# Down projection of four token tiles by seven block products instead of eight, weight sums by accumulating DMAs, the next modulation on TensorE

## The chip, the cores and the metric

The kernel runs on one core of a Trainium2 chip. A core has TensorE (PE, matrix products into PSUM), VectorE (DVE), ScalarE (ACT), GpSimd (POOL), SyncE (SP, which issues DMAs here) and 16 DMA engines. The metric is the time of one execution on the device, in microseconds (us); the kernel before takes 1401.62 us (median of three, 1400.32 to 1407.0).

## The reference

A two-layer network (D = 1024) works on 512 latent tokens and 128 context tokens. Each layer modulates and normalises, mixes tokens in four ways, and ends with a dense SwiGLU whose hidden width is 2816. The change lies in the last product and in the modulation that the next layer begins with:

```python
def modulation(cond, w_ada, b_ada):
    m = jax.nn.silu(cond) @ w_ada + b_ada
    ...
def swiglu(h, w_gate_up, w_down):
    g, u = jnp.split(h @ w_gate_up, 2, axis=-1)
    return (jax.nn.silu(g) * u) @ w_down
...
    h2 = rmsnorm(x, g_pre_ffn) * (1.0 + scale2) + shift2
    x = x + gate2 * rmsnorm(swiglu(h2, w_gate_up, w_down), g_post_ffn)
    return x, ckv, k_rope
```

The arithmetic is float32, with `w_down` of 2816 x 1024 for each layer.

## The kernel before, in words

**Products.** Every large product is three matmuls (`mm3`): each operand is split into a rounded part and a rest (`split`: ACT copies the rounded part, DVE subtracts it for the rest), and high x high, high x low and low x high are added in PSUM. A weight passes through `load`: SP issues a DMA into one of three `raw` buffers of 128 x 1024 float32 (512 KB), then ACT and DVE split it into one of eight `w` buffers. A `raw` buffer is free for the next DMA when its split has ended.

**Tokens.** The 640 tokens are five tiles of 128: 0 to 3 latent, 4 context. Hidden activations `hid` lie with the features on partitions: 22 slices of 128 features, tokens in the order 0 1 4 3 2. The last two slices are in a `w` buffer (`wk848` in layer 0).

**Down projection.** `w_down` makes the output in two halves of 512 columns. For each half, 11 loads of two slices are split, `hsplit` splits the two slices of all 640 tokens (128 x 1280), and five PSUM banks, one for each tile, collect 22 x 3 matmuls of 512 columns: 660 matmuls for a layer. In the second half the last three loads are kept (`tail`), so that the tiles end one after another. Behind each tile ACT squares and sums it, DVE multiplies it by the gate, POOL takes the root (`rsq`), DVE adds it to the residual (`postnorm`), SP stores it; in layer 0 the next norm (`prenorm`: ACT square, POOL root, two DVE scalings in `normalise`, eight transposes on TensorE) follows, and then the first products of the next layer's `w_in` (`pd`, 352 columns, in `pd_all`).

**Modulation.** The modulation of the next layer is made during layer 0's `w_down` by `queue_ada_v`: 16 steps, each one DMA of 512 KB into a `raw` buffer and two multiply-adds of 128 x 1024 on DVE; at the end of each half TensorE sums over partitions with four matmuls on `ones` and four transposes. In other places of the kernel the same kind of product is made on TensorE (`queue_gates`: 8 steps of four narrow matmuls, `ada_mm`, line 282).

**Order.** Instructions are written in the order in which TensorE is to run them. `clk` counts planned TensorE time, and background steps (`bg`) are put in at planned intervals; each engine runs its own queue in that order, with waits between queues. All DMAs of the kernel before are issued by SP, in order.

Of the kernel before, what the change touches and what calls it, by code (L numbers as in the profile page):

```python
# [10 lines left out]
F32 = mybir.dt.float32  # L11
R = mybir.dt.float32r
# [5 lines left out]
N = NS + NP  # L18
# [48 lines left out]
def layout(i):  # L67
# [21 lines left out]
    col = lambda v: np.repeat(v.reshape(L, 8, 128).transpose(0, 2, 1)[..., None], 2, 3).reshape(L, 128, 16)  # noqa: E731  # L89
# [30 lines left out]
    wd = a["w_down"].reshape(L, FF, 2, 512)  # L120
    o["w_dn"] = np.stack([kpack(wd[:, :, h], 2) for h in range(2)], 1)
# [6 lines left out]
# ---------------------------------------------------------------- chip  # L128
AFF = ("ssss", "aaaa")
START = (("aass",) * 5, ("aass",) * 5)  # L130
class Trunk:
    """The instructions are written in the order that the tensor engine runs them. A chain that has
    to wait for other engines is a generator: it yields the time (us of the tensor engine) until its
    next part is worth issuing, and the matmuls of other chains are issued meanwhile."""
# [8 lines left out]
    # -- order of issue  # L143
# [41 lines left out]
    # -- allocation  # L185
# [22 lines left out]
    # -- small things  # L208
# [13 lines left out]
    def mm3(self, out, l, r, start, stop):  # L222
        (lh, ll), (rh, rl) = l, r
        mm = self.nc.tensor.matmul
        mm(out, lh, rh, start=start, stop=False)  # L225
        mm(out, lh, rl, start=False, stop=False)  # L226
        mm(out, ll, rh, start=False, stop=stop)  # L227
# [13 lines left out]
    def rsq(self, ms, two=False):  # L241
        """(ms + eps)^-1/2 of each column, or of the sum of two."""
# [17 lines left out]
    # -- set-up  # L260
# [24 lines left out]
    def new_mod(self, l, r):  # L285
        """[shift, scale][k][c, c_ctx] of one norm, features on the partitions."""
# [50 lines left out]

    def queue_ada_v(self, l, r):
        """The same with the products on the vector engine; the tensor engine adds up the partitions."""
# [851 lines left out]
```

## Time and profile before

| what | before |
|---|---|
| time, median of three | 1401.62 us (1400.32 to 1407.0) |
| span of the profiled execution | 1403.1 us |
| PE busy | 1364.4 us (97%) |
| DVE busy | 1024.7 us (73%) |
| ACT busy | 620.6 us (44%) |
| POOL busy | 218.8 us (16%) |
| DMA | 180.61 MB, 129 GB/s on average |

The profiled execution is one run of the program; its span, from the first to the last instruction, is the only time of it that the profile has, and it stands 1.5 us above the median of the three timed runs. Busy times are of single engines and overlap. The granted clock is the clock of TensorE as a share of full speed. A line such as `L225 PE MATMUL ps<-w,hs` names the source line, the engine, the operation, and the tiles written and read; the time in square brackets is how long the engine had been idle, and what it waited for.

### The profile page before, as it was taken

The page shows a single profiled execution, that of the slowest core. Times are in us where ns is not written, and L with a number is a line of the kernel's source. Part 1 is how long each engine was busy: PE and PEld are TensorE (multiplying, and loading weights), DVE is VectorE, ACT ScalarE, POOL GpSimd, SP SyncE. Part 2 cuts the span into 40 slices and gives each one's busy share as a digit, 9 for nine tenths or more (in the row PEclk, how much of TensorE's full clock was granted, in tenths as well). Part 3 has the DMA queues.
Part 4 walks back from the last instruction along what each step waited for, and adds up shares of the span by engine and source line. Part 5 has one row for each costly group of instructions (what it writes and reads, how often), then busy time and mean ns, then how long its engine had stood idle before and what let it go on. Part 6 is the DMA issues. An engine that isn't in the chain of part 4 may idle for free. (4 is left out here: it accounts for less than half of the span.)

```text
span 1403.1 us, 21451 instructions
## 1 busy us (share of the span) xinstructions
PE 1364.4 (97%) x8320; PEld 1227.3 (87%) x8320; DVE 1024.7 (73%) x1722; ACT 620.6 (44%) x1210; POOL 218.8 (16%) x218
## 2 busy tenths in 40 slices
PE   5899999999999999999999999999999999999998
PEld 2788977899999999887888897878999999998886
DVE  3789476599988987978177966757998898782433
ACT  4543275564444444316173324736544444362410
POOL 1101121111222111000031202302021122140001
PEclk9999999999999999999999999999999999999999
DMA  9455246233222233655245533653122222342131
GB/s 374 164 173 184 91 143 236 98 114 99 85 88 76 91 91 108 194 181 166 85 155 167 183 115 122 189 188 135 61 90 91 91 90 77 106 135 77 59 105 75
DMA packets 50613, 180.61 MB, mean 129 GB/s; under 512 B 6784, under 2 KB 7680, under 8 KB 49488
## 3 DMA queue, kind: packets, MB, share of 16 engines
q1 hardware_dynamic: 50512, 179.25, 38.9%
q8 instruction: 65, 1.06, 0.3%
q14 instruction: 36, 0.29, 0.1%
HBM read 168.55 MB, written 10.68 MB: 128 GB/s over the span
## 5 line engine op out<-in xcount | busy, mean ns | idle before, releaser
L210 ACT ACTIVATE w<-raw 128x512 fp32r<-128x512 f32 (+2 forms) x228 | 186.4, 824 | 315.1 <-PE ps L227 204.0
L216 DVE TENSOR_TENSOR w<-raw,w 128x512 fp32r<-128x512 f32 (+2 forms) x228 | 215.9, 950 | 96.7 <-ACT w L210 93.5
L225 PE MATMUL ps<-T,w 128*128 128x320 f32 x640 | 197.8, 309 | 0.0
L226 PE MATMUL ps<-T,w 128*128 128x320 f32 x640 | 197.8, 309 | 0.0
L227 PE MATMUL ps<-T,w 128*128 128x320 f32 x640 | 197.8, 309 | 0.0
L225 PE MATMUL ps<-b,w 128*128 128x320 f32 x608 | 188.0, 309 | 0.0
L226 PE MATMUL ps<-b,w 128*128 128x320 f32 x608 | 187.9, 309 | 0.0
L227 PE MATMUL ps<-b,w 128*128 128x320 f32 x608 | 187.9, 309 | 0.0
L213 DVE TENSOR_TENSOR s<-ps,s 128x320 f32<-128x320 f32 (+1 forms) x304 | 142.3, 482 | 52.1 <-PE ps L227 50.8
L225 PE MATMUL ps<-w,hs 128*128 128x512 f32 x440 | 172.6, 392 | 0.2 <-ACT hs L210 0.2
L227 PE MATMUL ps<-w,hs 128*128 128x512 f32 x440 | 171.4, 390 | 0.3 <-DVE hs L216 0.3
L226 PE MATMUL ps<-w,hs 128*128 128x512 f32 x440 | 171.7, 390 | 0.0
L910 POOL TENSOR_TENSOR hid<-s 128x320 f32<-128x320 f32 x72 | 88.3, 1230 | 400.5 <-ACT s L210 369.6
L216 DVE TENSOR_TENSOR w<-sw,w 128x512 fp32r<-128x512 f32 x160 | 127.4, 814 | 0.0
L355 DVE SCALAR_TENSOR_TENSOR acc<-raw,cond,acc 128x1024 f32<-128x1024 f32 x84 | 108.4, 1318 | 17.9 <-DMA raw<-in_ada 17.9
L225 PEld LDWEIGHTS ps<-T,w 128*128 128x128 f32 x640 | 120.1, 188 | 0.0
L226 PEld LDWEIGHTS ps<-T,w 128*128 128x128 f32 x640 | 120.1, 188 | 0.0
L227 PEld LDWEIGHTS ps<-T,w 128*128 128x128 f32 x640 | 120.1, 188 | 0.0
L226 PEld LDWEIGHTS ps<-b,w 128*128 128x128 f32 x608 | 114.1, 188 | 0.1
L225 PEld LDWEIGHTS ps<-b,w 128*128 128x128 f32 x608 | 114.1, 188 | 0.1
L227 PEld LDWEIGHTS ps<-b,w 128*128 128x128 f32 x608 | 114.1, 188 | 0.0
L210 ACT ACTIVATE w<-sw 128x512 fp32r<-128x512 f32 x160 | 96.3, 622 | 34.7 <-PE ps L227 20.0
(219 smaller groups left out, 2674.0 us busy)
## 6 DMA issues: line engine op xcount, KB each, us to landing
raw<-in_w_gu SPq DMA_DIRECT2D x88, 512.0 KB, 3.5
raw<-in_ada SPq DMA_DIRECT2D x80, 512.0 KB, 4.1
raw<-in_w_dn SPq DMA_DIRECT2D x44, 512.0 KB, 3.6
ada<-in_ada SPq DMA_DIRECT2D x8, 1024.0 KB, 14.3
raw<-in_w_out SPq DMA_DIRECT2D x16, 512.0 KB, 4.9
xs<-work SPq DMA_DIRECT2D x14, 512.0 KB, 2.6
work<-xs SPq DMA_DIRECT2D x13, 512.0 KB, 4.4
raw<-in_w_b SPq DMA_DIRECT2D x12, 512.0 KB, 4.4
```

Source lines behind the costliest of these rows:

```text
L210: self.nc.scalar.activation(out, in_, f, **kw)
L213: self.nc.vector.tensor_tensor(out, x, y, op=op)
L216: self.nc.vector.tensor_tensor(lo, src, hi.bitcast(F32), op=ALU.subtract)
L225: mm(out, lh, rh, start=start, stop=False)
L226: mm(out, lh, rl, start=False, stop=False)
L227: mm(out, ll, rh, start=False, stop=stop)
L355: nc.vector.scalar_tensor_tensor(acc[:, s], raw, c, acc[:, s], op0=ALU.mult, op1=ALU.add)
L910: eng.tensor_tensor(h[:, ::-1] if c else h, x, y, op=ALU.mult)
```

## The change

`w_down` is written anew. The four latent tiles form two pairs, A (0, 1) and B (3, 2); the features form even and odd slices; the output has two halves. This 2 x 2 by 2 x 2 product is made by Winograd's form of Strassen's seven products, in seven passes over 11 slices (five groups of two slices and one of one slice, `w_dt`), and tile 4's plain products ride along in four of them: p1 (tiles 0, 1, 4), p5 (2 tiles), p6 (2), p3 (3), p7 (3), p2 (3), p4 (2): 18 tile products x 11 slices x 3 = 594 matmuls of 512 columns for a layer. Sums of weight blocks are made by accumulating DMAs, issued from GpSimd: `V`, in three `w` buffers, holds one block at p1 and is added to for p5, p6 and p4; for p7 a freshly loaded `raw` is added to and then split. Differences of activations are made on DVE (`dd`), partial sums in PSUM are copied by ACT (`cc`, `u2`) and added in `finish`. Tiles 0, 1 and 4 are finished early in p4 (`left`), tiles 3 and 2 at its end. In layer 0 `queue_ada_p` takes the place of `queue_ada_v`: 8 steps, each two DMAs of 512 KB and four narrow matmuls on TensorE, then four transposes. `pd_all` takes the tiles in the order 0, 1, 4, 3, 2. The host stores `w_down` by even and odd slices.

```diff
-                self.bg, self.bg_last = [(5.48, f) for f in q], self.now + 2.68
+                mod1, q = self.queue_ada_p(l + 1, 0)
+                self.bg, self.bg_last = [(8.0, f) for f in q], self.now + 8.0
...
-        for t in range(NT):
+        for t in (0, 1, 4, 3, 2):
             self.join(pre[t])
...
+        def add(dst, e, h, g):
+            nc.gpsimd.dma_start(out=dst, in_=dram(e, h, g), accum_op=ALU.add)
+
+        def fresh(g, e, h):
+            r = self.raw()[:, 0 : cnt(g) * 512]
+            nc.sync.dma_start(out=r, in_=dram(e, h, g))
+            return r
...
+        def p1(g):
+            into(g, 0, 0)
+            w = wsplit(g, vg(g))
+            add(vg(g), 0, 1, g)
+            h = xsplit(g, [x(g, 0)[:, :, A4]])
+            self.tt(d(g), x(g, 1)[:, :, D4], x(g, 0)[:, :, D4], ALU.subtract)
+            return h, w
+
+        go(p1, [(bA[0], 0, True, True), (bA[1], 128, True, True), (b4[0], 256, True, False)])
...
+        def p6(g):
+            w = wsplit(g, vg(g))
+            add(vg(g), 1, 0, g)
+            s = d(g)[:, :, 128:384]
+            nc.vector.scalar_tensor_tensor(s, s, -1.0, x(g, 0)[:, :, 0:256], op0=ALU.mult, op1=ALU.subtract)
+            return xsplit(g, [s]), w
...
+        def p7(g):
+            r = fresh(g, 0, 1)
+            add(r, 1, 1, g)
+            w = wsplit(g, r)
+            h = self.Q([2, 2, 384], R, "hs")
+            k = cnt(g)
+            s = self.S()[:, 0 : k * 256].rearrange("p (k n) -> p k n", k=k)
+            self.tt(s, x(g, 0)[:, :, 0:256], x(g, 0)[:, :, B4], ALU.subtract)
+            self.split(h[:, 0, 0:k, 0:256], h[:, 1, 0:k, 0:256], s)
+            self.split(h[:, 0, 0:k, 256:384], h[:, 1, 0:k, 256:384], x(g, 0)[:, :, 256:384])
+            return h, w
...
+        def left():
+            for t in (0, 1, 4):
+                begin(t)
+                if t < 4:
+                    finish(t, 0, bC[t], cc[:, 0, t, :])
+                else:
+                    finish(4, 0, b4[0])
+                end(t)
+
+        later.append(left)
+
+        def p4(g):
+            return xsplit(g, [x(g, 1)[:, :, B4]]), wsplit(g, vg(g))
+
+        steps = run(p4, [(bA[0], 0, None, True), (bA[1], 128, None, True)], tail=2)
```

On POOL, at the start of layer 0's down projection, the queue before held the last hidden products and then the roots of the tiles (`mso` are the sums of squares):

```order
L910 TENSOR_TENSOR wk848_5582<-s857_5624 128x5x64
L910 TENSOR_TENSOR wk848_5582<-s849_5583 128x320
L910 TENSOR_TENSOR wk848_5582<-s869_5745 128x5x64
L910 TENSOR_TENSOR wk848_5582<-s866_5716 128x320
L246 TENSOR_SCALAR rs1991_6724<-mso0885_5834 128x1
```

In the changed kernel the same stretch of POOL's queue begins so (`wk896`, `wk901` and `wk906` are the three buffers of `V`), and ends with the sums for p7:

```order
L944 TENSOR_TENSOR wk848_5582<-s857_5624 128x5x64
L944 TENSOR_TENSOR wk848_5582<-s849_5583 128x320
L1064 DMA wk896_5845<-in_w_dn 128x1024 x2
L944 TENSOR_TENSOR wk848_5582<-s869_5745 128x5x64
L1064 DMA wk901_5900<-in_w_dn 128x1024
L944 TENSOR_TENSOR wk848_5582<-s866_5716 128x320
L1064 DMA wk901_5900<-in_w_dn 128x1024
L1064 DMA wk906_5955<-in_w_dn 128x1024
L1064 DMA wk906_5955<-in_w_dt 128x512
```

24 sums now stand between the hidden products and the roots, and two hidden products of the last slice stand behind sums of p1.

On SP, in the middle of layer 0's down projection, weights and modulation shared the three `raw` buffers before, each released by DVE:

```order
L255 DMA raw936_6238<-in_w_dn 128x1024 [waits DMAHW5_49,DVE_49]
L349 DMA raw939_6252<-in_ada 128x1024 [waits DMAHW6_49,DVE_49]
L255 DMA raw940_6280<-in_w_dn 128x1024 [waits DMAHW7_49,DVE_49]
L349 DMA raw943_6291<-in_ada 128x1024 [waits DMAHW0_49,DVE_49]
L349 DMA raw944_6322<-in_ada 128x1024 [waits DMAHW1_49,DVE_49]
```

Now, at the end of p3 (`raw970` is its last group) and in p7 (`raw973`, `raw977`, `raw985`, `raw989`, `raw993` are its groups 0 to 4):

```order
L364 DMA raw968_6409<-in_ada 128x1024 [waits DMAHW2_49,PE_49]
L364 DMA raw969_6411<-in_ada 128x1024 [waits DMAHW3_49,DVE_49]
L1068 DMA raw970_6426<-in_w_dt 128x512 [waits DMAHW4_49,DVE_49]
L1068 DMA raw973_6444<-in_w_dn 128x1024 [waits DMAHW7_49,DVE_49]
L1068 DMA raw977_6475<-in_w_dn 128x1024 [waits DMAHW5_49,PE_49]
L364 DMA raw981_6491<-in_ada 128x1024 [waits DMAHW6_49,PE_49]
L364 DMA raw982_6493<-in_ada 128x1024 [waits DMAHW2_49,PE_49]
L1068 DMA raw985_6532<-in_w_dn 128x1024 [waits DMASW2_49,DVE_49]
L1068 DMA raw989_6563<-in_w_dn 128x1024 [waits DMASW3_49,DVE_49]
L1068 DMA raw993_6594<-in_w_dn 128x1024 [waits DMAHW3_49,PE_49]
```

`raw973` takes the buffer of `raw970` when DVE has split that; the modulation's buffers are now released by TensorE; `raw985` and `raw989` wait for the split of p7's first two groups, which wait for their sums (`DMASW`).

On DVE, at the end of layer 0's down projection, the chain of tile 0 (`work990`: gate, residual, the two scalings of the next norm) was followed by that of tile 1 (`work996`), with all weights split before it:

```order
L213 TENSOR_TENSOR work990_6720<-ps945_6336,gg875_5821 128x512 [waits Activation_49]
L876 SCALAR_TENSOR_TENSOR work990_6720<-t1884_5833,rt1992_6726,work990_6720 128x512 [waits DMAHW3_49,Pool_49]
L876 SCALAR_TENSOR_TENSOR work990_6720<-work990_6720,rt1992_6726 128x512 [waits DVE_49]
L397 TENSOR_SCALAR work990_6720<-work990_6720,rt1995_6738 128x512 [waits Activation_49,Pool_49]
L397 TENSOR_SCALAR work990_6720<-work990_6720,rt1995_6738 128x512
L213 TENSOR_TENSOR work996_6757<-ps946_6337,gg875_5821 128x512 [waits Activation_49]
```

Now three tiles' residuals (rows above these) and scalings (`work1025`, `work1028`, `work1031` are tiles 0, 1 and 4) stand ahead of the splits of p4's last three groups (`w1046`, `w1048`, `w1050`):

```order
L431 TENSOR_SCALAR work1025_6840<-work1025_6840,rt11038_6888 128x512 [waits Activation_49,Pool_49]
L431 TENSOR_SCALAR work1025_6840<-work1025_6840,rt11038_6888 128x512
L431 TENSOR_SCALAR work1028_6852<-work1028_6852,rt11041_6896 128x512 [waits Activation_49,Pool_49]
L431 TENSOR_SCALAR work1028_6852<-work1028_6852,rt11041_6896 128x512
L431 TENSOR_SCALAR work1031_6864<-work1031_6864,rt11044_6904 128x512 [waits Activation_49,Pool_49]
L431 TENSOR_SCALAR work1031_6864<-work1031_6864,rt11044_6904 128x512
L217 TENSOR_TENSOR w1046_6920<-wk901_5900,w1046_6920 128x1024
L217 TENSOR_TENSOR hs1047_6935<-hid498_2851,hs1047_6935 128x2x256 [waits PE_49]
L217 TENSOR_TENSOR w1048_6938<-wk906_5955,w1048_6938 128x1024 [waits DMASW0_49]
L217 TENSOR_TENSOR hs1049_6941<-wk848_5582,hs1049_6941 128x256
L217 TENSOR_TENSOR w1050_6944<-wk906_5955,w1050_6944 128x512 [waits DMASW1_49,PE_49]
```

The last three groups of weights are split behind three tiles' chains, and on TensorE 16 transposes of tiles 0 and 1, and the first of tile 4, stand behind the first two matmuls of the fourth group (`w1046`).

## Rows read from the trace of the kernel before

**Rows 1.** The page's line of busy times (share of the span, instructions), the start of its chain that ended last, and its DMA queues (packets, MB, share of 16 engines).

```profile
PE 1364.4 (97%) x8320; PEld 1227.3 (87%) x8320; DVE 1024.7 (73%) x1722; ACT 620.6 (44%) x1210; POOL 218.8 (16%) x218
...
q1 hardware_dynamic: 50512, 179.25, 38.9%
q8 instruction: 65, 1.06, 0.3%
q14 instruction: 36, 0.29, 0.1%
...
PE 40%; DVE 2%; DMA 2%; issue 1%; ACT 0%; POOL 0%; DVEq 0%; POOLq 0%; ACTq 0%
```

**Rows 2.** Busy time by stretches: start and end, length, then PE, PEld, DVE, ACT and POOL busy (instructions), granted clock, DMA share and GB/s. The first two are the down projections of layers 0 and 1; the last is a stretch of loading at the start of the program.

```profile
562.00:716.00 154.00, 153.29 (x692) 124.42 (x692) 104.36 (x107) 55.42 (x75) 8.04 (x12) 1.00 0.47 152
1246.00:1397.00 151.00, 150.38 (x665) 124.05 (x663) 61.41 (x57) 44.09 (x56) 16.63 (x10) 1.00 0.26 86
20.00:40.00 20.00, 17.04 (x88) 10.26 (x88) 9.79 (x25) 9.02 (x19) 0.29 (x1) 1.00 1.02 409
```

**Rows 3.** The timeline of TensorE (start, length, instruction): the first and the last matmuls of layer 1's down projection, with what follows the last on the way to the end of the program.

```profile
1246.44 0.39 PE L225 MATMUL ps<-w,hs 128*128 128x512 f32 x1
1246.67 0.39 PE L226 MATMUL ps<-w,hs 128*128 128x512 f32 x1
...
1396.00 0.39 PE L227 MATMUL ps<-w,hs 128*128 128x512 f32 x1
1396.42 0.60 ACT L210 ACTIVATE work<-ps 128x512 f32<-128x512 f32 x1 [3.39 <-PE ps L227]
...
1399.62 0.33 SPq L1045 DMA_DIRECT2D out_y_p<-work  x1
```

**Rows 4.** The timeline of TensorE at a modulation step made there (L282), and at the sum over partitions that `queue_ada_v` ends with (L364).

```profile
164.65 1.04 PE L364 MATMUL ps<-acc,ones 128*32 128x512 f32 x8
165.62 0.41 PE L225 MATMUL ps<-h,w 128*128 128x320 f32 x1
...
170.20 1.06 PE L282 MATMUL ps<-raw,cond 128*32 128x512 f32 x8
171.19 0.41 PE L225 MATMUL ps<-ql,w 96*128 96x320 f32 x1
```

**Rows 5.** DMA issues: what, how many, KB each, median us from issue to landing.

```profile
raw<-in_w_gu SPq DMA_DIRECT2D x88, 512.0 KB, 3.5
raw<-in_ada SPq DMA_DIRECT2D x80, 512.0 KB, 4.1
raw<-in_w_dn SPq DMA_DIRECT2D x44, 512.0 KB, 3.6
ada<-in_ada SPq DMA_DIRECT2D x8, 1024.0 KB, 14.3
xs<-work SPq DMA_DIRECT2D x14, 512.0 KB, 2.6
```

**Rows 6.** Groups of instructions of one form: count, then busy time, mean ns of one, and idle time before them.

```profile
L210 ACT ACTIVATE w<-raw 128x1024 fp32r<-128x1024 f32 x98 | 102.9, 1059 | 174.1 <-PE ps L227 66.2 <-DMA raw<-in_w_b 42.4 <-DMA raw<-in_w_dn 30.4
L216 DVE TENSOR_TENSOR w<-raw,w 128x1024 fp32r<-128x1024 f32 x98 | 120.9, 1240 | 70.5 <-ACT w L210 70.3
L216 DVE TENSOR_TENSOR w<-raw,w 128x512 fp32r<-128x512 f32 x120 | 85.5, 712 | 5.5 <-ACT w L210 2.6
L876 DVE SCALAR_TENSOR_TENSOR work<-work,rt 128x512 f32<-128x512 f32 x28 | 20.1, 746 | 0.8 <-POOL rt L250 0.8
L213 DVE TENSOR_TENSOR work<-ps,gg 128x512 f32<-128x512 f32 x28 | 19.3, 688 | 53.6 <-ACT work L210 53.6
L397 DVE TENSOR_SCALAR work<-work,rt 128x512 f32<-128x512 f32 x38 | 16.8, 484 | 34.0 <-POOL rt L250 33.2 <-ACT pdt L210 0.8
```

**Rows 7.** The timeline of TensorE around the end of layer 0's down projection (first transposes of a tile, the wait for the third tile, the matmuls behind it, first products of the next layer), and below it the same engine by stretches of 2 us (PE busy, granted clock, DMA share, GB/s).

```profile
711.50 1.06 PE L238 MATMUL ps<-ident,work 128*128 128x128 f32 x8
712.32 0.47 PE L225 MATMUL ps<-w,hs 128*128 128x512 f32 x1
...
716.28 0.39 PE L227 MATMUL ps<-w,hs 128*128 128x512 f32 x1
718.53 1.71 PE L238 MATMUL ps<-ident,wk 128*128 128x128 f32 x8 [1.85 <-DVE wk L397]
...
720.89 0.63 PE L227 MATMUL ps<-w,hs 128*128 128x512 f32 x1
...
723.14 0.32 PE L225 MATMUL ps<-w,h 128*128 128x352 f32 x1
723.29 0.32 PE L226 MATMUL ps<-w,h 128*128 128x352 f32 x1
...
718.00:720.00 2.00, 1.47 (x9) 0.71 1.01 344
720.00:722.00 2.00, 2.00 (x7) 0.50 0.74 303
722.00:724.00 2.00, 2.00 (x11) 0.93 0.86 283
```

**Rows 8.** POOL's hidden products: the page's group of all of them (count, busy time, mean ns), and the timeline of POOL at the start of layer 1's down projection.

```profile
L910 POOL TENSOR_TENSOR hid<-s 128x320 f32<-128x320 f32 x72 | 88.3, 1230 | 400.5 <-ACT s L210 369.6 <-DVE s L213 30.9
...
1247.68 13.18 POOL L910 TENSOR_TENSOR wk<-s 128x320 f32<-128x320 f32 x2 [10.28 <-ACT s L210]
```

More of the change, by code (lines that the diff above doesn't have):

```diff
@@ new lines, in w_down, with x, d, dram @@
+        pre, later = [None] * NT, []
+        cnt = lambda g: 2 if g < 5 else 1
+        A4, B4, D4 = slice(0, 384), slice(384, 640), slice(256, 640)
+        TILE = {0: 0, 1: 128, 4: 256, 3: 384, 2: 512}
+        dd = [self.Q([3, 2, 384], F32, "dd") for _ in range(2)]
+        V = [None] * 3
+        def x(g, e):
+            return hid[g].rearrange("p (k e) n -> p k e n", e=2)[:, :, e]
+        def d(g):
+            return dd[g // 3][:, g % 3, 0 : cnt(g)]
+        def dram(e, h, g):
+            return a["w_dn"][l, e, h, g] if g < 5 else a["w_dt"][l, e, h]
@@ new lines, in wsplit, with xsplit @@
+        def wsplit(g, s):
+            w = self.wp.tile([128, 2, 1024], R, tag="w", name=self.nm("w"))
+            n = cnt(g) * 512
+            self.split(w[:, 0, :n], w[:, 1, :n], s)
+            return w
+        def xsplit(g, parts):
+            n = sum(v.shape[2] for v in parts)
+            h = self.Q([2, 2, 384], R, "hs")
+            o = 0
+            for v in parts:
+                m = v.shape[2]
+                self.split(h[:, 0, 0 : cnt(g), o : o + m], h[:, 1, 0 : cnt(g), o : o + m], v)
+                o += m
+            return h
@@ new lines, in mms, with run @@
+        def mms(g, k, h, w, outs, first, last):
+            for ps, o in outs:
+                self.mm3(ps, (h[:, 0, k, o : o + 128], h[:, 1, k, o : o + 128]), self.wk(w, slice(k * 512, k * 512 + 512)),
+                         bool(first) and g == 0 and k == 0, last and g == NG - 1 and k == cnt(g) - 1, first is None)
+        def run(make, outs, tail=0):
+            kept = []
+            for g in range(NG):
+                h, w = make(g)
+                if g >= NG - tail:
+                    kept.append((g, h, w))
+                else:
+                    for k in range(cnt(g)):
+                        for ps, o, first, last in outs:
+                            mms(g, k, h, w, [(ps, o)], first, last)
+                if g == 1:
+                    while later:
+                        later.pop(0)()
+            for ps, o, first, last, done in [(*q, None) if len(q) == 4 else q for q in (outs if tail else [])]:
+                for g, h, w in kept:
+                    for k in range(cnt(g)):
+                        mms(g, k, h, w, [(ps, o)], first, last)
+                yield
@@ new lines, in go, with finish @@
+        def go(make, outs):
+            for _ in run(make, outs):
+                pass
+        cc = self.Q([2, 2, 512], F32, "cc")
+        def finish(t, half, ps, other=None, neg=False):
+            g = gg[t // 4][:, half * 512 : half * 512 + 512]
+            dst = t1[:, t, :] if half else works[t][:, 0:512]
+            if other is None:
+                self.evac(ps, dst, g, mss[t], half)
+                return
+            self.tt(other, ps, other, ALU.add)
+            self.act(dst, other, AF.Square, scale=1 / 32.0, accum_out=mss[t][:, half : half + 1])
+            if neg:
+                nc.vector.scalar_tensor_tensor(dst, other, -1.0, g, op0=ALU.mult, op1=ALU.mult)
+            else:
+                self.tt(dst, other, g, ALU.mult)
@@ new lines, in w_down, with begin, end @@
+        works = {}
+        def begin(t):
+            works[t] = self.W() if t == 2 else self.Q([2048], F32, "work")
+            self.load_x(src, t, works[t])
+        def end(t):
+            work = works[t]
+            xt = work[:, 1024:2048]
+            self.postnorm(xt, work[:, 0:512], t1[:, t, :], mss[t])
+            if nxt is not None:
+                pre[t] = self.spawn(self.prenorm(t, work, nxt[0], self.mix_sink(nxt[1]), 5.97))
+                dst = nxt[2][t]
+            else:
+                dst = a["y_p"] if t == 4 else a["y_s"][t * 128 : t * 128 + 128, :]
+            nc.sync.dma_start(out=dst, in_=xt)
@@ new lines, in left @@
+        def left():
[3 more added lines that the diff above has]
+                    finish(t, 0, bC[t], cc[:, 0, t, :])
+                else:
+                    finish(4, 0, b4[0])
[4 more added lines that the diff above has]
+        steps = run(p4, [(bA[0], 0, None, True), (bA[1], 128, None, True)], tail=2)
+        for p, t in enumerate((3, 2)):
+            next(steps)
+            begin(t)
+            finish(t, 0, bA[p])
+            end(t)
```

120 lines of the change are left out of this document (71 added, 49 removed).

## The prediction

> **What bounds the kernel now.** I read the page's busy line and its chain first [rows 1]: TensorE is busy 97% of the span and has 40% of the chain that ended last, where every other engine has 2% or less. What is taken off TensorE is therefore gained, as long as nothing else becomes late. Next the stretches of the two down projections [rows 2]: TensorE is busy 153.3 of 154 us and 150.4 of 151 us at a clock of 1.00, while DVE has 104.4 and 61.4 us of work and the DMA engines are used at 0.47 and 0.26. There is room beside TensorE, more in layer 1 than in layer 0, where DVE makes the next modulation. Then TensorE's timeline in layer 1 [rows 3]: the first matmul starts at 1246.44, the last at 1396.00, and 659 starts in 149.56 us are 0.227 us for a matmul of 512 columns. The end of the program hangs on the last of them: 3.6 us to the store of the last tile, which the change leaves as it is.
>
> **The matmuls removed.** 660 become 594 in each layer, 66 x 0.227 = 15.0 us, 30.0 us for both. The seven-product form removes TensorE's work only; the copies and differences that it adds are on ACT, DVE and the DMA queues.
>
> **The modulation moved to TensorE (layer 0).** A step on TensorE takes 170.20 to 171.19, 0.99 us [rows 4], and eight take 7.9. Removed are two sums over partitions of 0.97 us (164.65 to 165.62) and four of eight transposes of about 0.1 (eight of them stand from 711.50 to 712.32 [rows 7]), 2.4 together. That adds 5.5 us. With both terms alone the time would be 1401.6 - 30.0 + 5.5 = 1377.1. (The terms come from the profiled execution; its span of 1403.1 is 0.1% over the median, so I take them off the median.)
>
> **The split weights and differences on DVE and ACT.** A full group needs on DVE 1.24 us for the weights' rest; in p6 it also needs a difference of two 256-column slices (0.75) and their rest (0.71) [rows 6], 2.70 together. TensorE takes 12 x 0.227 = 2.72 for it. This is the tightest pass; p5 needs 1.95 of 2.72, p3 and p7 about 3.0 of 18 x 0.227 = 4.08, p2 2.2. Splits may run some groups ahead (eight `w` buffers less three for V and those of `hid`), so I cost these at nothing. If the cover is gone, a tenth more on DVE in p6 costs 5.5 x 0.25 = 1.4 us for a layer.
>
> **The sums by DMA.** No row shows an accumulating DMA, nor any that POOL issued: all traffic is on the queue of SP's DMAs but for two small ones [rows 1, 5]. So the duration X of a sum of 512 KB, from issue to landing, is bounded by neighbours: 2.6 us is the shortest of its size (a store), 14.3 us the longest median, for 1024 KB in a crowd [rows 5]. A plain load of w_down takes 3.6; a sum has to read its destination as well, which at the highest rate seen, 409 GB/s [rows 2], is 1.3 us more. I take X = 4.9, near the load's row. Passes p5 and p6 ask for one sum in 2.72 us, by two readings at 409 GB/s 2.6 us: it just fits, and p1 before them (22 us for 5.5 groups) gives a lead. The Trainium skill (Collectives: The Full Stack, "Why ReduceScatter is half of AllGather") says the same of the reduce: it is slow because the add needs two source reads, not because adding takes cycles. By that rule the engine time doubles, and the sum comes out as above; no row here shows it.
>
> **p7 in layer 0, where I expect the wait.** Only here does a sum stand between a load and its split: load 3.6, sum 4.9, split 1.06 + 1.24 = 2.3 [rows 5, 6], 10.8 us for a `raw` buffer. There are three, shared with the modulation, whose buffers are now freed by TensorE only. With t = 0 at the start of p3: the load of p3's fifth group takes a buffer that TensorE frees in the third group, t = 11.0 (two groups, one step of 0.99, a third of a group, half a step). It lands at 14.6 and is split at 16.9; that buffer takes the last group, landed 20.5, split (half width, about 1.3) 21.8; that buffer takes p7's first, landed 25.4, summed 30.3, split 32.6. TensorE wants it at 5.5 x 4.08 + 3.5 x 0.99 = 25.9. It waits 6.7 us. The third group of p7 takes that buffer again: 32.6 + 10.8 = 43.4, wanted at 32.6 + 8.16 + 0.9 = 41.7, another 1.7 to 2. I take 8.7 for both. Queued behind the waiting split on ACT and DVE are p7's other splits and differences and the ends of two tiles, all for TensorE's later rows; behind the waiting load on SP the second group's load and the modulation's last two; behind the waiting sum on POOL only sums of p7. So nothing gets ahead meanwhile. In layer 1 the ring has no modulation: 10.8 / 3 = 3.6 us for a group against 4.08, no wait.
>
> **What a wait costs beside itself.** In layer 0's tail TensorE stands 1.85 us, and behind it matmuls of 512 columns last 0.63 us where they last 0.39 elsewhere; the clock is granted at 0.71, 0.50 and 0.93 in the next three stretches of 2 us [rows 7], half speed (1.2 GHz) for most of it: 0.6 + 1.0 + 0.1 = 1.7 us lost. Two waits in p7 add 3.4.
>
> **The tail of layer 0.** DVE makes, from the end of p2: two sums with `cc` (1.4), one split (0.7), three tiles of 0.69 + 2 x 0.75 (6.6), six scalings of 0.48 (2.9), then the weights of p4's fourth group (1.2) [rows 6]: 12.8 us. TensorE has for it 38 matmuls (8.6) and 17 transposes (1.8): it waits 2.4. Before, the wait for the third tile (1.85 and its clock) stood in the same tail, and now p4's end and three tiles of `pd` (24 x 0.155 = 3.7 us each, 723.14 to 723.29 [rows 7]) cover the chains of tiles 3 and 2. Net +1. At the worst the wait of before stays as well and both lose clock: +6. For layer 1's end, where the load of the last tile's residual stands behind two stores on SP, +1 (0 to 2.6, a store's row).
>
> **Sum.** 1377.1 + 8.7 + 3.4 + 1 + 1 = 1391.2 us. I forecast 1391.
>
> **Rivals.**
> 1. *Sums late (slower).* Place: p7 in both layers. The time follows X: both waits in layer 0 grow with it, 2 x (X - 4.9); in layer 1 a group takes (X + 5.9)/3, more than 4.08 from X = 6.3, and loses 5.5 x ((X + 5.9)/3 - 4.08) = 1.83 X - 11.6. The time is 1391.2 + 2 (X - 4.9) + 1.83 X - 11.6: it is even with the kernel before at X = 8.3, 1409 at 10, 1425 at 14.3; at 2.6 it would be 1386 (the second wait gone, the first 4.4). For it: POOL has to issue these DMAs between its own work, and two of its products, 1.23 us each elsewhere, took 13.2 us together at the start of layer 1's down projection, while DVE was busy [rows 8]; in p6 and p7 DVE is dense. Against: the sums of p1, which stand beside such products, have 20 us of lead. The Trainium skill (SBUF — State Buffer, "Who interferes with whom") has a rule that goes against this change: a DMA issued by GpSimd starves when DVE holds the port that its descriptors need, but for `tensor_tensor`, which takes the reading side only, it infers no such block. By the rule p7, mostly `tensor_tensor`, is not touched; rows 8 agree as to reading, and none shows an issue.
> 2. *All hidden.* The ring runs further ahead than I count and p7 has its first two groups in time: 1377 to 1382. For it: DMA at 0.26 to 0.47 and ACT mostly idle in these stretches [rows 2]. Against: the chain of buffers above, each released by the one before, leaves no slack at X of 3 or more.
> 3. *The tail.* DVE in layer 0's tail takes over: three tiles now at once beside p4's splits, +6 there instead of +1, and as much again if the last quarter of `w_pd`, whose load stands on SP behind a store, comes late by 3.6 and halves the clock: 1396 to 1402. For it: the wait of 1.85 stands there already [rows 7]. Against: `pd` of three tiles hides the last two chains.
>
> That TensorE's work is not removed can't be: the order has 118 rows fewer on it.
>
> **Chances.** Forecast (1385 to 1396) 0.46, late sums from 1396 up 0.25, all hidden 0.14, the tail 0.15. A measurement of this kernel can tell about 0.5% (7 us) from no change: faster is under 1394.6, slower over 1408.6. Faster: 0.40 of the forecast, all of the hidden case, 0.01 of the tail: 0.55. Same: 0.06 of the forecast, 0.11 of the tail, 0.07 of the late sums: 0.24. Slower: 0.18 of the late sums (X over about 10) and 0.03 of a tail with more than counted: 0.21. The likeliest case's own range is 1385 to 1396; the range for 8 in 10 goes from 1377 to 1414, which takes in X up to 11.
>
> **What would show it.** TensorE's matmuls of both down projections at 0.227 us and 594 of them; waits of TensorE on the split of `w` in p7 of layer 0, one near 7 us and one near 2, with the clock halved behind each, and hardly any in layer 1. The issue table would give X for the sums: under 6 is the forecast, over 8 the first rival. Waits in p5, p6 or p4 for sums would show that the engines' rate, and not p7's chain, decides, and that would make the prediction wrong; so would long waits on POOL's roots or on transposes in the tail.

## The result, and the profile after

The changed kernel takes 1413.23 us (median of five) against 1404.79 us of the kernel before beside it: the ratio is 1.0076, with a 95% interval of 1.0058 to 1.0093. By the ratio it is slower by about 11 us; one of the five executions of the kernel before took 7662.8 us and does not enter the ratio, which is why the two medians are only 8.4 us apart. The prediction was 1391 and faster. The profiled execution has a span of 1415.2 us, 12.1 over that of the kernel before; it lies 3.8 us over the median of its five.

The page after; the first lines answer to [rows 1]:

```profile
PE 1354.4 (96%) x8232; PEld 1210.9 (86%) x8232; DVE 1066.9 (75%) x1840; ACT 662.2 (47%) x1313; POOL 248.9 (18%) x266
...
q1 hardware_dynamic: 51088, 179.25, 38.4%
q0 software_dynamic: 6912, 23.07, 9.2%
...
wk<-in_w_dn POOLq DMA_DIRECT2D x30, 512.0 KB, 7.4
raw<-in_w_dn SPq DMA_DIRECT2D x30, 512.0 KB, 4.0
```

TensorE is busy 10 us less, yet the span is 12 us longer. A sum of 512 KB takes 7.4 us from issue to landing (median), a plain load of `w_down` 4.0.

Where the time went is read from TensorE's timeline, by the first matmul of each kind (start, length, instruction). After:

```profile
561.16 0.39 PE L227 MATMUL ps<-w,hs 128*128 128x512 f32 x1
...
731.06 0.32 PE L227 MATMUL ps<-w,h 128*128 128x352 f32 x1
...
762.36 0.32 PE L229 MATMUL ps<-w,h 128*128 128x352 f32 x1
...
994.61 0.31 PE L227 MATMUL ps<-b,w 128*128 128x320 f32 x1
...
1270.03 0.39 PE L227 MATMUL ps<-w,hs 128*128 128x512 f32 x1
...
1407.55 0.39 PE L229 MATMUL ps<-w,hs 128*128 128x512 f32 x1
```

In the kernel before two of these marks stand in no row shown so far, the last `pd` matmul and the first of layer 1's gate and up product (the others are in [rows 3] and [rows 7], the first `hs` matmul of layer 0 at 562.26):

```profile
745.59 0.32 PE L227 MATMUL ps<-w,h 128*128 128x352 f32 x1
...
971.02 0.30 PE L225 MATMUL ps<-b,w 128*128 128x320 f32 x1
```

The differences of the marks:

| stretch of TensorE | before | after | change | foretold |
|---|---|---|---|---|
| up to layer 0's down projection | 562.3 | 561.2 | -1.1 | 0 |
| down projection of layer 0, to the first `pd` matmul | 160.9 | 169.9 | +9.0 | +3.6 |
| first products of layer 1 (`pd`) | 22.5 | 31.3 | +8.8 | 0 |
| rest of layer 1's token mixing | 225.4 | 232.2 | +6.8 | 0 |
| gate and up of layer 1 | 275.4 | 275.4 | 0 | 0 |
| down projection of layer 1 | 149.6 | 137.5 | -12.0 | -15.0 |
| behind the last matmul | 7.1 | 7.6 | +0.5 | +1 |

Row by row the changes miss what was foretold by -1.1, 5.4, 8.8, 6.8, 0, 3.0 and -0.5, 22.4 us in all. The first is no effect of the change: over the twelve profiled executions of this document that stretch, whose code is the same in all, ends between 559.1 and 563.3 us.

Layer 1 has most of its gain. Layer 0 gives back twice as much, and two thirds of that outside the passes. TensorE's waits after, added up by what they waited for (us in total, times, longest; the first row, left out, is a wait of 11.1 us for `ada` that both kernels have):

```profile
...
PE ps L228 <- DVE w L217: 10.6, 8, 4.9
PE ps L227 <- ACT w L211: 8.4, 4, 3.8
PE ps L240 <- ACT s L211: 8.4, 4, 6.4
...
```

The long ones stand in these places (TensorE's timeline after):

```profile
649.40 1.05 PE L284 MATMUL ps<-raw,cond 128*32 128x512 f32 x4 [1.98 <-DMA raw<-in_ada]
654.20 1.65 PE L227 MATMUL ps<-w,hs 128*128 128x512 f32 x3 [3.75 <-ACT w L211]
669.12 1.65 PE L227 MATMUL ps<-w,hs 128*128 128x512 f32 x3 [2.92 <-ACT w L211]
...
736.40 0.43 PE L228 MATMUL ps<-w,h 128*128 128x352 f32 x1 [4.86 <-DVE w L217]
...
826.71 0.47 PE L240 MATMUL ps<-ident,s 128*128 128x128 f32 x1 [6.45 <-ACT s L211]
```

The first three are p7's beginning and its third group, as foretold. The other two were not: the first `pd` product of the next layer waits for the split of `w_pd`, and, 64 us behind the last of them, transposes in the Fourier part wait for ACT. The long waits cost clock as well. By stretches (PE, PEld, DVE, ACT, POOL busy, granted clock, DMA share, GB/s), p3 to p7 and the tail after, then the same stretch and the tail before:

```profile
640.00:680.00 40.00, 31.35 (x119) 22.04 (x118) 16.08 (x28) 12.30 (x21) 5.30 (x6) 0.83 0.75 186
720.00:760.00 40.00, 32.01 (x169) 29.21 (x168) 32.61 (x69) 24.62 (x61) 7.72 (x15) 0.87 0.48 164
```

```profile
640.00:680.00 40.00, 39.67 (x180) 31.62 (x179) 25.59 (x27) 20.42 (x24) 0.00 (x0) 1.00 0.42 128
716.00:760.00 44.00, 42.04 (x234) 37.84 (x234) 37.91 (x84) 25.07 (x72) 14.77 (x20) 0.96 0.50 164
```

A mean of 0.83 over 40 us, between full speed and half, is 13 to 14 us at 1.2 GHz.

### The profile page after: what moved, and what is told of

Its sections match the earlier page's. It is cut to its first block, busy times and chain, and to the rows that moved or that the text cites. A ratio compares the mean times of both kernels' runs of the same rounds, so it can differ in the third digit from the quotient of the medians.

```text
span 1415.2 us, 21657 instructions
## 1 busy us (share of the span) xinstructions
PE 1354.4 (96%) x8232; PEld 1210.9 (86%) x8232; DVE 1066.9 (75%) x1840; ACT 662.2 (47%) x1313; POOL 248.9 (18%) x266
## 3 DMA queue, kind: packets, MB, share of 16 engines
q1 hardware_dynamic: 51088, 179.25, 38.4%
q0 software_dynamic: 6912, 23.07, 9.2%
## 4 chain that ended last, share of the span: by engine, by line
PE 75%; DMA 9%; DVE 6%; issue 3%; ACT 2%; POOL 2%; POOLq 0%; DVEq 0%; SPq 0%; ACTq 0%
PE ps L227 23%; PE ps L228 23%; PE ps L229 23%; DMA raw<-in_w_dn 4%; PE ps L240 3%; DMA raw<-in_ada 2%; DVE acc L389 2%; PE ps L284 2%; DVE w L217 2%; ACT w L211 1%; DMA raw<-in_w_out 1%; PE ps L822 1%; DMA raw<-in_w_b 1%; POOL rt L252 1%; POOL rs L248 1%
## 5 line engine op out<-in xcount | busy, mean ns | idle before, releaser
L211 ACT ACTIVATE w<-raw 128x512 fp32r<-128x512 f32 (+2 forms) x220 | 175.8, 803 | 248.3 <-PE ps L229 126.9
L217 DVE TENSOR_TENSOR w<-raw,w 128x512 fp32r<-128x512 f32 (+2 forms) x220 | 202.3, 922 | 75.3 <-ACT w L211 72.3
L227 PE MATMUL ps<-w,hs 128*128 128x512 f32 x396 | 157.5, 400 | 6.8 <-ACT w L211 6.7
L228 PE MATMUL ps<-w,hs 128*128 128x512 f32 x396 | 157.0, 396 | 2.6 <-DVE w L217 2.6
L229 PE MATMUL ps<-w,hs 128*128 128x512 f32 x396 | 156.8, 396 | 0.6 <-DVE hs L217 0.6
L227 PEld LDWEIGHTS ps<-w,hs 128*128 128x128 f32 x396 | 75.7, 192 | 30.6 <-ACT w L211 8.0
```

Source lines behind the costliest of these rows:

```text
L211: self.nc.scalar.activation(out, in_, f, **kw)
L217: self.nc.vector.tensor_tensor(lo, src, hi.bitcast(F32), op=ALU.subtract)
L227: mm(out, lh, rh, start=start, stop=False, skip_group_check=more)
L228: mm(out, lh, rl, start=False, stop=False, skip_group_check=more)
L229: mm(out, ll, rh, start=False, stop=stop, skip_group_check=more)
```

## The experiments

Three theories for the loss in layer 0: R, the ring of three `raw` buffers, shared with the modulation, makes the waits inside the passes; D, the order on DVE makes the wait at `pd`; D2, DVE is full in the tail whatever its order. The rival to R is S: the sums' rate holds the passes. For the token mixing behind there was no theory yet.

**The modulation back on DVE.**

```diff
-                mod1, q = self.queue_ada_p(l + 1, 0)
-                self.bg, self.bg_last = [(8.0, f) for f in q], self.now + 8.0
+                mod1, q = self.queue_ada_v(l + 1, 0)
+                self.bg, self.bg_last = [(5.48, f) for f in q], self.now + 2.68
```

> The changed kernel with the next modulation back on DVE (queue_ada_v, as before). Theory R (the ring of three raw buffers, held by modulation steps that only TensorE frees, makes the waits inside the passes): the two waits for raw<-in_ada (3.7 us) and 5.5 us of modulation go from TensorE, but DVE gets 32 instructions of about 1.3 us (41 us) into passes where it has little room, so new waits on splits of w; 1403 to 1413. Rival S (the passes are held by the rate of the sums, whatever shares the ring): the waits stay, only the 5.5 us go: about 1408, with the waits in p7 as large as now (3.8 and 3.1 us). Told apart by the waits in p3 and p7.

1421.27 us, ratio 1.0137 (1.0112 to 1.0162): worse than the changed kernel, outside what either theory gave. From the start of the passes to 680 us DVE is busy 100.5 of 121 us, where the changed kernel has 70.4 of 120:

```profile
559.00:680.00 121.00, 103.39 (x427) 79.10 (x426) 100.53 (x121) 49.13 (x72) 21.45 (x24) 0.96 0.83 202
...
PE ps L227 <- ACT w L211: 14.7, 6, 5.7
```

The waits for split weights grow from 8.4 to 14.7 us, in six for four, and those for split activations (`hs`) from 0.8 to 8.2. So in layer 0 the seven products go worse with the old modulation than with the new. Whether DVE or the ring does it, the run does not tell: the kernel before has DVE busy for 94.1 of the same 121 us and no long wait there, and ACT, whose copies of the weights TensorE waits for, itself waits for DMAs into `raw` (7.19, 3.65 and 7.68 us), where the old modulation's loads stand as well.

**The modulation on TensorE alone, in the kernel before.** The edit above the other way round, with the old `w_down`.

> The kernel before with the modulation on TensorE alone (queue_ada_p, interval 8.0). If the modulation costs what it adds on TensorE: 1402 + 5.5 = 1407 to 1408. If its buffers in the ring cost waits even beside plain loads: 1410 to 1416. If the 41 us that it takes off DVE are worth more than it adds: under 1402.

1409.09 us, ratio 1.0050 (1.0031 to 1.0069), 7 us (4 to 10). The first `pd` matmul comes 166.1 us after the first `hs` matmul for 160.9, +5.2, close to the 5.5 foretold. Two kernels further down, whose layer 0 is that of the kernel before, take 159.7 and 159.4 us for the same stretch; against them it is 6.4 and 6.7. So the term was about right, its buffers cost nothing beside plain loads (TensorE's waits in the stretch are 2.7 us for 2.6), and what it takes off DVE is worth nothing there.

**Modulation steps earlier.**

```diff
-                self.bg, self.bg_last = [(8.0, f) for f in q], self.now + 8.0
+                self.bg, self.bg_last = [(5.5, f) for f in q], self.now + 5.5
```

> The changed kernel with one number changed: modulation steps every 5.5 us for 8.0, so that all eight are done in p1 to p6 (52 us), where no weight passes through raw, and the ring belongs to p3, p7 and p2 afterwards. Theory R: the waits in the passes (1.6, 2.1, 3.8, 3.1 us) and about 5 us of halved clock behind them mostly go; with sums of 7.4 us a buffer of p7 takes 4.0 + 7.4 + 2.3 = 13.7 us, 4.6 for a group against 4.08, so 1 to 3 us stay: 1398 to 1403. Rival S: the waits in p7 stay at 7 us: 1409 to 1413.

1411.95 us, ratio 1.0069 (1.0046 to 1.0092). The profile and the time say different things, and both matter. The down projection of layer 0 falls from 169.9 to 160.0 us and no wait in p3 or p7 is longer than 1 us: theory R holds there, and S falls. But the expected 1398 to 1403 did not come, and the interval of the ratio covers that of the changed kernel: `pd` still takes 30.9 us and the rest of the mixing 232.2, and in this execution layer 1's passes took 141.9 us for 137.5, with a wait of 3.4 us in p7. The spans differ by 4.7 us, and most of that is the profiled execution of the changed kernel, which lies 3.8 us over its median.

**The splits of `w_pd` earlier.**

```diff
             next(steps)
+            if t == 3 and nxt is not None:
+                self.first_pd(l + 1)
+                self.more_pd(l + 1)
             begin(t)
...
-                self.first_pd(l + 1)
-                self.more_pd(l + 1)
```

> The changed kernel with the loads and splits of w_pd written ahead of the ends of tiles 3 and 2 (they stand behind them now, though the data is there 30 us earlier). Theory D (the order on DVE makes the wait at the first matmuls of the next layer): the waits of 5.0 and 1.8 us there and about 3 us of halved clock go, 1403 to 1406. Rival: DVE is simply full in this stretch, and the wait moves to the transposes or splits of tiles 3 and 2: 1409 to 1413.

1410.39 us, ratio 1.0053 (1.0030 to 1.0076), not told apart from the changed kernel. The wait of 4.9 us at the first `pd` product becomes 1.25, and 14 us later a new one stands, of nearly the same size, at the transposes of tile 2:

```profile
729.08 0.43 PE L228 MATMUL ps<-w,h 128*128 128x352 f32 x1 [1.25 <-DVE w L217]
...
738.77 0.32 PE L229 MATMUL ps<-w,h 128*128 128x352 f32 x1
743.23 1.97 PE L240 MATMUL ps<-ident,wk 128*128 128x128 f32 x8 [4.14 <-DVE wk L431]
744.85 0.64 PE L227 MATMUL ps<-w,h 128*128 128x352 f32 x1
```

From the first to the last `pd` matmul it is 31.0 us as before the edit (31.3). Theory D named the wait, but not the limit: as the rival has it, the wait moves. The rows show one more thing: TensorE stands before the transposes of tile 2 with 48 of the 120 `pd` matmuls done, and the products of the third tile (tile 4, transposed at 724.5) stand behind them in its queue.

**Seven products in layer 1 alone.** Layer 0 gets the old `w_down`, the modulation on DVE and the old order of tiles.

```diff
-            pre = self.w_down(l, x, hid, gg, nxt)
+            pre = (self.w_down if l else self.w_down_plain)(l, x, hid, gg, nxt)
```

> Layer 0 as in the kernel before (plain product, modulation on DVE, tiles in the old order), layer 1 with the seven products and the sums by DMA. If the loss lies in what layer 0 puts around the passes (modulation in the ring, tail with the next norm, order of the next mixer), layer 1 keeps its 8 to 12 us: 1390 to 1395 against 1402. Rival: the passes themselves lose (late sums, p7's ring, the tail) and layer 1's gain in the profile is paid elsewhere: 1399 to 1404.

1394.37 us, ratio 0.9933 (0.9910 to 0.9956): faster than the kernel before, by 6 to 13 us. The passes, the sums and p7's chain are the same in layer 1 as in layer 0; the loss lies in what layer 0 has around them.

**p7 without its sums.**

```diff
             r = fresh(g, 0, 1)
-            add(r, 1, 1, g)
             w = wsplit(g, r)
```

> The changed kernel without the accumulating DMAs of p7 (12 of 48; the second block is left out of p7's weights). Load, sum, split of 13.7 us becomes load and split of 6.3 us. If the chain through the sum makes p7's waits in layer 0 (3.8 and 3.1 us), both go, and so do layer 1's waits in p7 (0.8 us in the profile); the wait of 2.1 us for the modulation's load ahead of p7 stays: 1401 to 1407. If the ring alone makes them (buffers held by the modulation), the first wait stays at 2 to 4 us and the time is 1408 to 1413.

One execution, 1400.42 us, with the second block missing from p7's weights. The waits of 3.75, 2.92 and 1.98 us go; the longest left in p7 is

```profile
648.81 0.50 PE L227 MATMUL ps<-w,hs 128*128 128x512 f32 x1 [0.65 <-ACT w L211]
...
654.41 1.06 PE L284 MATMUL ps<-raw,cond 128*32 128x512 f32 x8
```

The wait for the modulation's load ahead of p7 goes too, which I had not expected. That load comes no sooner (SP issues it at 644.90, in the changed kernel at 644.25), but the step that reads it stands elsewhere in TensorE's queue: in the changed kernel half of it stood ahead of p7's first matmul, here all of it stands behind the first group. So another order came with the edit, and not the sums alone made that wait. Layer 0's passes take 155.7 us (169.9) and layer 1's 136.2 (137.5). In layer 0 p7 waits where two things meet, buffers that the modulation holds and a sum between load and split; taking away either took these waits. A sum alone can still make one: layer 1 has no modulation, and its p7 waits 0.6 to 3.4 us.

**The scalings of the next norm on ACT**, on top of the early modulation steps.

```diff
         for hf in range(2):
+            if on_act:
+                self.act(work[:, hf * 512 : hf * 512 + 512], work[:, 1024 + hf * 512 : 1536 + hf * 512], AF.Identity, scale=r)
+                continue
             self.nc.vector.tensor_scalar(work[:, hf * 512 : hf * 512 + 512], work[:, 1024 + hf * 512 : 1536 + hf * 512], r, None, op0=ALU.mult)
...
-        self.normalise(work)
+        self.normalise(work, wait == 5.97)
```

> The kernel with early modulation steps (interval 5.5), and the scalings of the next norm behind layer 0's down projection (ten of 0.48 us) on ACT for DVE. If DVE is full in this tail (theory D2: work of DVE, not its order, sets the end of the first products of the next layer), 4.8 us less on DVE take 3 to 6 us off the 31 us from the first to the last of these matmuls and off the waits at the transposes: 1405 to 1409 against 1412. Rival: the order alone makes the wait (w_pd's split behind the ends of tiles 3 and 2), its 5 us stay, the time too: 1410 to 1413.

1403.35 us, ratio 1.0002 (0.9982 to 1.0022): 8.6 us under the kernel without this edit (the intervals do not touch), more than expected, and from another place. The `pd` stretch still takes 30.6 us, with its waits now on ACT's scalings: D2 in its simple form, DVE's load, falls as well; DVE is busy there for 24.3 of 31 us in the changed kernel and was for 19.5 of 23 before. What fell is the rest of the mixing, from 232.2 to 221.7 us. Some 59 us behind the last `pd` matmul, far from the edit, the wait at the Fourier transposes is 1.76 us for 6.51:

```profile
813.36 0.33 PE L240 MATMUL ps<-ident,s 128*128 128x128 f32 x1 [1.76 <-ACT s L211]
```

There DVE's order differs. In the kernel before, and in this one, both multiply-adds of a modulation step stand together between two Fourier steps (`y` and `s`); the rows are of the kernel before:

```
L216 TENSOR_TENSOR y451115_7534<-s1126_7630,y451115_7534 128x512
...
L213 TENSOR_TENSOR s1131_7668<-ps1128_7658,s1130_7666 128x255 x2
L355 SCALAR_TENSOR_TENSOR acc1143_7726<-raw1171_7964,cond_81,acc1143_7726 128x1024 x2
```

In the changed kernel the first of the two stands ahead of these steps and the second behind them, and the split of the next `w` behind that:

```
L389 SCALAR_TENSOR_TENSOR acc1186_7842<-raw1214_8080,cond_81,acc1186_7842 128x1024
L217 TENSOR_TENSOR y451158_7650<-s1169_7746,y451158_7650 128x512
...
L214 TENSOR_TENSOR s1174_7784<-ps1171_7774,s1173_7782 128x255 x2
L389 SCALAR_TENSOR_TENSOR acc1186_7842<-raw1214_8080,cond_81,acc1186_7842 128x1024
L217 TENSOR_TENSOR w1218_8113<-raw1217_8111,w1218_8113 128x1024
```

What follows from it is seen in the changed kernel's timeline. The second multiply-add ends at 821.9 and frees its `raw`; only then SP can load the next weights; ACT, in order, stands at their split and makes the copy `s` that TensorE waits for only afterwards:

```profile
820.67 1.27 DVE L389 SCALAR_TENSOR_TENSOR acc<-raw,cond,acc 128x1024 f32<-128x1024 f32 x1
...
821.97 0.33 SPq L257 DMA_DIRECT2D raw<-in_w_b  x1
...
825.11 1.06 ACT L211 ACTIVATE w<-raw 128x1024 fp32r<-128x1024 f32 x1 [3.16 <-DMA raw<-in_w_b]
826.08 0.58 ACT L211 ACTIVATE s<-ps 128x512 f32<-128x512 f32 x1
```

**Three mends together, in layer 1 alone and in both layers.** In layer 1 the ends of tiles 0, 1 and 4 are written behind p4's last split, and two groups of p7 are summed in a `w` buffer; the scalings go to ACT. The kernel with both layers has the early modulation steps and the early splits of `w_pd` as well, and `at=NG - 1` in layer 1 alone.

```diff
-                if g == 1:
+                if g == at:
                     while later:
...
+            if g in (2, 3):
+                if g == 2:
+                    wide.append(self.W())
+                r = wide[0][:, (g - 2) * 1024 : (g - 1) * 1024]
+                nc.sync.dma_start(out=r, in_=dram(0, 1, g))
+            else:
+                r = fresh(g, 0, 1)
...
-        steps = run(p4, [(bA[0], 0, None, True), (bA[1], 128, None, True)], tail=2)
+        steps = run(p4, [(bA[0], 0, None, True), (bA[1], 128, None, True)], tail=2, at=NG - 1 if l else 1)
```

> Seven products in layer 1 alone, with three mends: the scalings of the next norm behind layer 0's down projection on ACT; in layer 1 the ends of tiles 0, 1 and 4 written behind the last split of p4 (wait of 1.6 us there); the third and fourth group of p7 summed in a w buffer, so that four buffers go round for three (13.7 / 4 = 3.4 us for a group against 4.08; wait of 3.3 us there). If these are the waits that are left: 4 us in layer 1 and 2 to 4 in and behind the tail of layer 0 go, 1386 to 1390 against 1394 without them. If each only gives way to the next one: 1392 to 1395.

> Seven products in both layers, modulation steps every 5.5 us, w_pd's splits ahead of the ends of tiles 3 and 2, the scalings on ACT, and the two mends of p7 and p4's end. If the tail of layer 0 is DVE's (full from the end of p2 on, whatever its order), the first products of the next layer still take some 30 us for 22 and the time stays at 1396 to 1402; if the order of w_pd's split was what was left, 8 us go there: 1388 to 1393.

Both missed: 1406.15 us, ratio 1.0025 (1.0010 to 1.0040), and 1420.57 us, ratio 1.0120 (1.0100 to 1.0141). In the first DVE's order in the mixing has turned into that of the changed kernel, and so has the wait; and with the `w` buffer for p7's sums the wait there is longer, 5.50 us for 3.11 in the run without it:

```profile
812.21 0.48 PE L242 MATMUL ps<-ident,s 128*128 128x128 f32 x1 [6.46 <-ACT s L213]
...
1341.58 0.79 PE L229 MATMUL ps<-w,hs 128*128 128x512 f32 x1 [5.50 <-ACT w L213]
```

The scalings on ACT, which had come with a good order in one program, came with a bad one in this, and the wait went with the order both times; the `pd` stretch in layer 0, where the scalings stand, is 26.9 us for 23.4 without them. So the gain was the order's, not ACT's. In the second, the `pd` stretch is 34.7 us, and p7 of layer 0 waits again, where early steps alone had left nothing over 1 us:

```profile
669.32 0.79 PE L227 MATMUL ps<-w,hs 128*128 128x512 f32 x1 [6.08 <-ACT w L211]
```

**The end of p4 alone.** Seven products in layer 1 alone, and of the mends only `at=NG - 1` for p4.

> Seven products in layer 1 alone (as e6_layer1_only), and there only the ends of tiles 0, 1 and 4 written behind the last split of p4. DVE's order in layer 1's mixer is that of the kernel before, so its wait for a transpose stays at 1 to 3 us (in the kernel e10_best, with the other order, it was 6.6). If the wait of 1.6 us at p4's fourth group is a matter of that order alone it goes: 1391 to 1394 against 1394. If the end of the last tiles comes later by as much: no change. A time over 1398 would mean that the loss of e10_best lies in this mend.

1390.57 us, ratio 0.9926 (0.9904 to 0.9949): the lowest time here, 7 to 13 us under the kernel before. The wait of 1.4 us at p4's fourth group is gone; layer 1's passes take from 1242.13 to 1380.76, 138.6 us, for 142.1 without the mend, and half of that difference is a shorter wait in p7 (1.41 us for 3.11). What the mend is worth in time is not shown: its interval and that of the kernel without it (0.9910 to 0.9956) lie almost on one another.

## Why the prediction was wrong

The measured time lies inside the widest range, which went to 1414. That is luck: the width was for sums of up to 11 us, and they took 7.4.

**Right: the matmuls and the modulation.** Layer 1's passes fell by 12.0 us of 15.0 (a wait of 1.4 at p4's fourth group and one of 0.6 in p7 were not foretold), and the modulation alone cost 5.2 in its stretch and 7 in time, for 5.5. One reading ahead of these terms was wrong, without harm to them: the chain of [rows 1], followed back, begins at 752.56 us, so TensorE's 40% in it says nothing of layer 0's down projection.

**Right: p7's chain.** "It waits 6.7 us", then "another 1.7 to 2", 8.7 together. Measured: 1.98 and 3.75 at its beginning and 2.92 at the third group, 8.7. The two experiments that took away the modulation's share of the ring and the sums took these waits away. Two of its terms were off and made up for one another: a sum takes 7.4 us (median) for the 4.9 taken, and part of the first wait is for the modulation's own load. One more wait for a modulation load, 1.5 us in p3, was not foretold.

**Too small: the price of a wait in clock.** "Two waits in p7 add 3.4." Behind them the granted clock is 0.50 from 654.20 to 658.20 and from 669.12 to 675.20, so 2.0 and 3.0 us are lost for 1.7 each. Over all, the clock is 0.83 in the mean from 640 to 680 us, up to 0.17 x 40 = 6.8 us, and 0.87 over the 40 us of the tail, 5.2, for 1.8 before (0.04 x 44); part of this ran while TensorE waited, so these are upper bounds. The waits were more, and half clock stood behind the long ones.

**Wrong: the tail of layer 0.** "Net +1", because "`pd` of three tiles hides the last two chains". This is the step that failed first. Its 2.4 us inside p4 came (0.57, 0.51 and 1.20). But `pd` took 8.8 us more. I had seen the split of `w_pd` only as a late load on SP (rival 3); its load was issued at 693 us, and the split stood on DVE behind the residual of tile 3 and the gate of tile 2 (timeline after, SP and DVE):

```profile
693.31 5.09 SPq L257 DMA_DIRECT2D raw<-in_w_pd  x3
...
733.54 0.75 DVE L910 SCALAR_TENSOR_TENSOR work<-work,rt 128x512 f32<-128x512 f32 x1
...
734.86 0.68 DVE L214 TENSOR_TENSOR wk<-ps,gg 128x512 f32<-128x512 f32 x1
735.47 0.88 DVE L217 TENSOR_TENSOR w<-raw,w 128x704 fp32r<-128x704 f32 x1
```

Nor is that order the limit: with the splits ahead, tile 2's transposes waited instead; with ten scalings on ACT, those waited. In all three forms, and in the kernel with modulation on DVE, the stretch is 30.6 to 31.4 us.

In the changed kernel the 8.8 us are two waits for splits of `w_pd`, 4.86 and 1.42, and half clock around the second (0.50 from 736.73 to 743.50, some 2.7 us). What the forms share is seen from the last tile: the last matmul of the down projection and the transposes of the tile that ends there, after and then before.

```profile
730.83 0.39 PE L229 MATMUL ps<-w,hs 128*128 128x512 f32 x1
...
747.40 1.03 PE L240 MATMUL ps<-ident,wk 128*128 128x128 f32 x8
```

```profile
722.91 0.39 PE L227 MATMUL ps<-w,hs 128*128 128x512 f32 x1
...
731.67 1.09 PE L238 MATMUL ps<-ident,work 128*128 128x128 f32 x8
```

From one to the other it is 16.6 us for 8.8 (16.1 to 17.2 in the other runs with seven products in layer 0, 21.5 in the one with three mends), and from these transposes to the last `pd` matmul another 14 to 15 us pass in every kernel. (The changed kernel comes to them without a wait, held up by `w_pd`; the form with the early splits waits 4.14 us there.) The forecast set 72 `pd` matmuls, three tiles, against the last chains. In TensorE's queue only 39 stand ahead of these transposes, 48 in the forms with the early split or with ACT, 46 in the kernel before. So the cover was no longer than before, while the way to the transposes took twice the time. Two causes are open, and neither was tried alone: the order on TensorE, which puts the transposes ahead of products that are ready, and the way the tiles end. In the old form the tiles end one in 4.08 us of matmuls, so one chain runs while the next tile is multiplied; in the new, three tiles end at once with p2 and two 2 us apart with p4. That this staggering makes the chain long fits all runs, but no run restored it within the seven products, so it is argued, not shown.

**Missing: the token mixing behind.** This was no term of the sum: I took the program behind the change to be as before, since its code is. The stretch grew by 6.8 us, and 3.9 of it is one wait, 6.45 us for 2.52, which comes with another order of DVE's queue. Over all twelve kernels with a profile the wait at the Fourier transposes goes with this order: 1.3 to 2.5 us in the five with the order of before, 5.8 to 6.5 in the seven with the other. It does not go with the seven products: the run with ACT's scalings has them in layer 0 and the order of before, the first of the three-mend kernels has the plain product there and the other order. Why the build chose one or the other was not looked into. The rest of the 6.8 us is clock and smaller waits; the whole stretch overlaps, 221.7 to 226.4 us with the order of before and 225.6 to 232.2 with the other.

**The rivals.** Late sums, the rival on the other side, was priced at 1398 for X = 7.4 and would not have made the kernel slower. (Its formula gives 1408 at X = 10, not 1409.) Its place was right: without p7's sums the one execution took 13 us less. But that is the 12.1 us which the forecast had already charged there (8.7 and 3.4), and the 1400.4 us that are left without them are no gain over the kernel before: the rest lies in the tail and behind it. The tail, rival 3, was nearest in place: it was given 5 to 11 us over the forecast, and `pd` took 8.8, but by another chain than the load on SP. Of POOL held up by DVE there is no sign: its eight `wk` products, four of them beside the sums, took 1.03 us in the mean (0.87 to 1.53), and a sum 0.89 to issue:

```profile
L1064 POOL DMA_DIRECT2D wk<-in_w_dn x30 | 26.7, 891 | 65.6 <-DVE w L217 50.5 <-PE ps L229 8.0 <-DVE hs L217 3.8
...
L944 POOL TENSOR_TENSOR wk<-s 128x320 f32<-128x320 f32 x8 | 8.3, 1032 | 29.1 <-ACT s L211 23.3 <-DVE s L214 5.8
```

The rule from the Trainium skill (SBUF — State Buffer, "Who interferes with whom") that GpSimd's DMAs can starve was thus not seen at work in these passes, where `tensor_tensor` is most of DVE's work, as the rule itself infers.

What stays open: what of the tail's 8.8 us is staggering and what the order on TensorE; and why layer 1's passes vary, 137.5 to 142.1 us between kernels with the same code there, with a wait in p7 of 0.6 to 3.4 us behind a sum.

## What to carry to other kernels

Here a form with fewer products was worth it in the last layer, where no next layer hangs on the order in which its results end (ratios 0.9933 and 0.9926, some 10 us), and not in the layer whose tail feeds the next. Count buffers by who frees them: a ring shared by loads, in-place sums and an operand that the bound engine itself reads makes that engine wait for its own progress. Before a product is counted as cover for a chain, look where the end of that chain stands in the engine's queue. After any change, compare the order of the queues in the code that was not changed; a build can pay there for what was gained elsewhere.

## What was not expected of the hardware

An accumulating DMA is dear in engine time. The sums moved 23.07 MB in 9.2% of the span of 16 engines (130 us of 1415.2), 2.96 us for 512 KB; all other loads and stores moved 179.25 MB in 38.4%, 1.59 us for 512 KB. That is a ratio of 1.86 (the kernel with sums in layer 1 alone has 11.54 MB in 4.7% of 1393.0 us, 2.98 us for 512 KB), and the engines were full (share 1.00) in the first 38 us of layer 0's passes while only 211 GB/s were moved, where plain loads at the start of the program fill them (1.02) with 409 [rows 2]:

```profile
562.00:600.00 38.00, 38.00 (x178) 28.72 (x176) 28.73 (x34) 15.71 (x22) 12.01 (x13) 1.00 1.00 211
```

The rule of the Trainium skill (Collectives: The Full Stack, "Why ReduceScatter is half of AllGather"), told there of a collective's reduce, is that the add needs two source reads and so has half the rate; this ratio nearly agrees.
